# Value projections of a decoder trunk: two Strassen passes in place of one pass and direct products

## The chip, the cores and the metric

The kernel runs on one core of a Trainium2 chip. The metric is the device time of one execution in microseconds (us), as the median of several runs. Engines: TensorE (PE) multiplies, VectorE (DVE) and ScalarE (ACT) do the elementwise work, GpSimd (POOL) a little of it, SyncE (SP) issues most DMAs; ScalarE issues some as well. Each engine works through its own instructions in order.

## The reference, cut to what matters

One layer, 1024 tokens of 1024 channels, all in float32. A combined projection gives queries, keys and values of a differential attention (A: 4 heads, 512 value columns) and of three dilated window groups (B: 3 groups of 4 heads, 1536 value columns), and 2048 gate columns:

```
h    = rms_norm(x, pre_mix_g[l])
proj = h @ w_in[l]
qa, ka, va, qb, kb, vb, gates = jnp.split(proj, split_at, axis=-1)
...                                   # rope on q and k
oa   = diff_attention(qa, ka, va, lam)
outs, lses = dilated_group(qb[:, :, g], kb[:, :, g], vb[:, :, g], window, dil)   # g = 0, 1, 2
ob   = softmax of the lses over g, times outs
g_a, g_b = jnp.split(jax.nn.sigmoid(gates), 2, axis=-1)
mix  = (g_a * (norm(oa) @ w_a_out) + g_b * (ob @ w_b_out)) @ w_mix_out
x    = x + rms_norm(mix, post_mix_g[l])
```

A convolutional gated MLP with a second residual follows; the change leaves it alone.

## The kernel before, in words

**Products.** Every float32 matrix is split into a high part in TensorE's reduced float format (ScalarE copies it, name ending in `h` or `whi`) and a low part (VectorE subtracts, `l` or `wlo`). A product is then three matmuls, high times high, low times high and high times low (`mm3`, lines 153 to 156). So one block of 128x128 by 128x512 costs three matmuls of 128x512, one copy of the high part and one subtraction per weight tile.

**The x operand.** `xh` and `xl` hold x transposed, scaled by the norm's channel gain, as 8 chunks of 128 channels by 1024 tokens. The norm's own factor per token (`rstd`) is put in when results leave the PSUM banks.

**The start.** While x arrives in the order `K_FIRST` (chunks 0, 4, 1, 5, ...), PE does three of the sixteen gate projections, `FIRST_GATES`, k by k into six banks: 8 chunks x 6 banks x 3 = 144 matmuls of 128x512. Beside it VectorE and ScalarE form the sums of quadrants of x that Strassen's method needs (`sums_x`: t2, t3, t4 and the difference whose negative is b12).

**The Strassen pass.** For 1024 of the 2048 value columns (B groups 1 and 2) the 1024x1024 product of tokens and columns is done with seven products of halves, in Winograd's form (`order_v`: p1, p5, p6, p7, p3, p2, p4). A product is 4 steps, one for each k, of 12 matmuls; step n's weight (a quadrant of w_v or a sum of quadrants) is loaded 8 steps ahead (`fetch_v`), summed and split 5 steps ahead (`ready_v`). Quadrants and sums used again stay in the tiles `wa` and `wz`. Products take turns on the left banks (three `acc` and `o`) and the right ones (two `s` and two `pt`). After its last step, `take_v` (lines 497 to 512) copies or adds the four banks into the SBUF tiles `yv`, the four quarters of the result. These are scaled by `rstd` and stored to `v_d` in DRAM (`store_v`). During the pass the norm of x is computed (`norm_x`: 16 loads of raw x, 16 squares with a sum on ScalarE), and the rotary tables.

**The other 1024 value columns** (A, and B group 0) are projected directly by `proj_v` (lines 568 to 588): for 256 columns, 8 token tiles x 8 k x 3 = 192 matmuls of 128x256 (lines 577 to 579), four such calls. One runs in the start, after two more gates and the first head's projections; one in heads 1 and 2 of attention A, one in head 3 and one in the middle of B.

**Fill.** Attention steps wait for softmax, which is VectorE's and ScalarE's work. So `interleave` mixes other matmuls between them: a fill is a generator that gives up after every half unit, and it is spread over the jobs of a head by weight. `A_FILLS` names the fills of each A head: `p` and `P` the next projections of queries and keys, `g` one gate (48 matmuls), `v`, `w` and `V` the direct value projections. The B steps have the projections of the next step, and `ahead`, a value projection, in steps 4 and 5. The last `B_GATES` = 3 gates are fill after B.

**Order.** Engines run in the order in which a scheduler placed the program's instructions, and tiles come from pools with a fixed number of buffers, so a load waits until its buffer's last reader is done. All weight loads go through SP's queue in order; the stores of `v_d` through ScalarE's.

## Time and profile before

| what | value |
|---|---|
| median of 3 runs | 1745.36 us (1737.62 to 1745.58) |
| profiled execution | 1742.07 us, span 1740.3 us |
| mean granted TensorE clock | 0.992 |
| PE busy | 1709.9 us, 98% of the span |
| DVE busy | 1350.6 us, 78% |
| ACT busy | 886.3 us, 51% |
| DMA | 201.79 MB, mean 116 GB/s |
| raw loads of w_v | 24 of 256 KB |

The page gives busy times by engine and by group of instructions; a group's mean duration counts from issue to end, and since matmuls overlap, the sum of their durations is longer than the time they occupy. A window's row in the table by stages gives, for each engine, the time in which it had at least one instruction under way, with the number of instructions, then the clock granted to TensorE (1.00 is full), the share of DMA time and the rate in GB/s. An idle time is listed in brackets with what ended it.

### The profile page before, as it was taken

To read this page: it belongs to the slowest core of one execution; us is meant where nothing else is said; L and a number is where in the kernel's file an instruction comes from. 1 tells how busy PE (TensorE), PEld (TensorE's weight loads), DVE (VectorE), ACT (ScalarE), POOL (GpSimd) and SP (SyncE) were. 2 spreads that over 40 slices of the span, in tenths; PEclk is the share of its full clock that TensorE was granted. 3 is DMA by queue.
4 is the path that set the end of the run, shared out by engine and by line. 5 is a ranking of instruction groups with operands and counts; after the bars stand their busy time and mean duration, and the time that the engine had idled before them with its cause. 6 is when DMAs were issued, how large, how long until landed. Compare 5 with 4: busy or idle time off the path is not lost.

```text
span 1740.3 us, 23773 instructions
## 1 busy us (share of the span) xinstructions
PE 1709.9 (98%) x8510; PEld 1445.5 (83%) x8510; DVE 1350.6 (78%) x2642; ACT 886.3 (51%) x1629; POOL 54.4 (3%) x78
## 2 busy tenths in 40 slices
PE   9999999999999999999999999999999999999997
PEld 7878878898998888888877888878888888878886
DVE  8794677777757665777655767899999999789978
ACT  6654465555436674567652433354444444355452
POOL 1000000000000000000000500300000000000000
PEclk9999999999999999999999999999999999999999
DMA  5753101122112213422375532122222222196624
GB/s 208 237 182 123 53 26 66 56 80 90 38 62 73 84 51 117 153 85 74 123 267 189 185 119 98 37 91 97 79 97 79 79 91 97 56 345 209 206 79 157
DMA packets 103494, 201.79 MB, mean 116 GB/s; under 512 B 16768, under 2 KB 21568, under 8 KB 103376
## 3 DMA queue, kind: packets, MB, share of 16 engines
q1 hardware_dynamic: 97328, 189.26, 32.6%
q10 hardware_dynamic: 6048, 11.01, 1.7%
q8 instruction: 67, 1.10, 0.3%
q14 instruction: 51, 0.42, 0.1%
HBM read 156.57 MB, written 43.66 MB: 115 GB/s over the span
## 4 chain that ended last, share of the span: by engine, by line
PE 82%; DVE 7%; DMA 6%; ACT 2%; issue 2%; SPq 1%; POOL 0%; DVEq 0%; ACTq 0%; POOLq 0%
PE acc L155 16%; PE acc L154 16%; PE acc L156 16%; PE acc L1460 3%; PE acc L1459 3%; PE acc L1458 3%; PE o L634 2%; DMA og<-og_d 2%; PE pt L621 2%; PE acc L1139 2%; PE acc L1140 2%; PE acc L1138 2%; PE acc L578 2%; PE acc L577 2%; PE acc L579 2%
## 5 line engine op out<-in xcount | busy, mean ns | idle before, releaser
L154 PE MATMUL acc<-xh,whi 128*128 128x512 f32 x744 | 297.8, 401 | 6.2 <-ACT xh L358 2.6
L155 PE MATMUL acc<-xh,wlo 128*128 128x512 f32 x744 | 296.7, 399 | 0.9 <-DVE wlo L147 0.9
L156 PE MATMUL acc<-xl,whi 128*128 128x512 f32 x744 | 294.6, 398 | 0.0
L150 ACT ACTIVATE whi<-raw 128x512 fp32r<-128x512 f32 (+1 forms) x250 | 153.9, 624 | 226.3 <-PE acc L156 145.5
L147 DVE TENSOR_TENSOR wlo<-raw,whi 128x512 fp32r<-128x512 f32 (+1 forms) x247 | 174.7, 714 | 50.2 <-ACT whi L150 49.2
L154 PEld LDWEIGHTS acc<-xh,whi 128*128 128x128 f32 x744 | 141.3, 190 | 35.2 <-ACT xh L358 3.7
L155 PEld LDWEIGHTS acc<-xh,wlo 128*128 128x128 f32 x744 | 141.6, 190 | 27.9 <-DVE wlo L147 1.1
L156 PEld LDWEIGHTS acc<-xl,whi 128*128 128x128 f32 x744 | 141.5, 190 | 27.7
L154 PE MATMUL acc<-mh,whi 128*128 128x512 f32 x400 | 155.7, 390 | 0.3 <-ACT mh L150 0.2
L155 PE MATMUL acc<-mh,wlo 128*128 128x512 f32 x400 | 155.6, 389 | 0.0
L156 PE MATMUL acc<-ml,whi 128*128 128x512 f32 x400 | 155.4, 389 | 0.0
L608 ACT ACTIVATE t<-acc 64x512 f32<-64x512 f32 (+1 forms) x160 | 94.6, 591 | 47.9 <-PE acc L156 45.8
L1336 DVE TENSOR_TENSOR u<-acc,u 128x512 f32<-128x512 f32 x133 | 90.8, 687 | 26.4 <-PE acc L156 26.4
L150 ACT ACTIVATE whi<-s 128x512 fp32r<-128x512 f32 x76 | 47.0, 628 | 108.3 <-PE acc L156 96.0
L609 DVE TENSOR_TENSOR t<-acc,cos 128x512 f32<-128x512 f32 x64 | 44.1, 689 | 65.5 <-ACT t L608 63.2
L154 PEld LDWEIGHTS acc<-mh,whi 128*128 128x128 f32 x400 | 75.1, 188 | 16.2 <-ACT mh L150 0.5
L156 PEld LDWEIGHTS acc<-ml,whi 128*128 128x128 f32 x400 | 75.1, 188 | 15.6
L155 PEld LDWEIGHTS acc<-mh,wlo 128*128 128x128 f32 x400 | 75.1, 188 | 15.6
L1459 PE MATMUL acc<-whi,wlo 128*128 128x512 f32 x220 | 77.3, 389 | 0.0
L1458 PE MATMUL acc<-whi 128*128 128x512 f32 x220 | 75.8, 389 | 0.0
L578 PE MATMUL acc<-whi,xl 128*128 128x256 f32 x256 | 73.6, 288 | 0.0
L579 PE MATMUL acc<-wlo,xh 128*128 128x256 f32 x256 | 73.5, 287 | 0.0
(404 smaller groups left out, 4101.0 us busy)
## 6 DMA issues: line engine op xcount, KB each, us to landing
raw<-in_w_in SPq DMA_DIRECT2D x110, 256.0 KB, 2.7
raw<-in_w_up SPq DMA_DIRECT2D x88, 256.0 KB, 2.7
raw<-c_d SPq DMA_DIRECT2D x48, 256.0 KB, 3.3
c_d<-c SPq DMA_DIRECT2D x22, 512.0 KB, 2.7
raw<-in_w_down SPq DMA_DIRECT2D x37, 256.0 KB, 3.5
gl<-gt_d SPq DMA_DIRECT2D x16, 512.0 KB, 5.1
gt_d<-gate ACTq DMA_DIRECT2D x26, 256.0 KB, 2.4
raw<-in_w_v SPq DMA_DIRECT2D x24, 256.0 KB, 3.4
```

Source lines behind the costliest of these rows:

```text
L147: eng.tensor_tensor(lo, src, hi.bitcast(F32), op=ALU.subtract)
L150: nc.scalar.activation(hi, src, AF.Copy)
L154: nc.tensor.matmul(o, sh, mh, start=first, stop=False)
L155: nc.tensor.matmul(o, sl, mh, start=False, stop=False)
L156: nc.tensor.matmul(o, sh, ml, start=False, stop=last)
L578: nc.tensor.matmul(ps, xl[:, k, tk], wh[:, w], start=False, stop=False)
L579: nc.tensor.matmul(ps, xh[:, k, tk], wl[:, w], start=False, stop=k == KC - 1)
L608: nc.scalar.activation(t1[dst], ps[src], AF.Copy)
L1336: nc.vector.tensor_tensor(to, made(p), x, op=ALU.add)
L1458: nc.tensor.matmul(banks[m], gh[:, tk], wh, start=f == 0, stop=False)
L1459: nc.tensor.matmul(banks[m], gl[:, tk], wh, start=False, stop=False)
L1460: nc.tensor.matmul(banks[m], gh[:, tk], wl, start=False, stop=f == NH - 1)
```

## The change

- All 2048 value columns go through the Strassen method, in two passes (i = 0 and 1) of 1024 columns; `v_d` is twice as wide and holds them all. `proj_v` is gone, with its 768 matmuls of 128x256.
- The passes begin where the first gates stood: 12 steps of products p1 and p2 (p1 and p2 of pass 0 in turn, then p2 of pass 1), in the order in which the first chunks of x arrive. Then come p5, p6, p7, p4, p3 of pass 0, and p1, p5, p6, p7, p4, p3 of pass 1: 56 steps of 12 matmuls.
- Sums stay in the banks: the left banks go from p1 through p6 and p7 to p4 without being cleared, the right ones from p2 or p5 to p3. `take_v` copies the running sum out between two products, and the next product adds on top. Copies of p6, p7, p4 are ScalarE's; the rest is added by VectorE.
- No weight quadrant is kept in `wa`; each product loads what it needs, 72 raw loads of w_v in place of 24.
- The norm of x comes at step 16 (during p6 of pass 0), the rotary angles at 30, their tables at 53. Stores of pass 0 are at steps 26, 29, 33, 36; two quarters of pass 1 are stored through SP's queue.
- Attention reads all its values back from `v_d` (`fetch_values`, `split_values`): two tiles of 128x1024 with one split each for 256 columns.
- All sixteen gates are ordinary ones: one in the start, three in each A head (`A_FILLS`), three after B. `v`, `w` and `V` remain in the lists but hold no matmuls.

The core of the diff:

```diff
-START_GATES, A_FILLS, B_GATES = 2, ("gpgg", "pvgg", "wpgg", "PVg"), 3
+START_GATES, A_FILLS, B_GATES = 1, ("gpgg", "gpvgg", "wgpgg", "gPVgg"), 3
...
-FIRST_GATES = (0, 1, 2)
-XT_BUFS, NORM_AT, ANGLES_AT, STORE_AT = 6, 4, 18, 26
+XT_BUFS, NORM_AT, ANGLES_AT, TABLES_AT, STORE_AT = 6, 16, 30, 53, {26: 0, 29: 3, 33: 2, 36: 1}
...
-        order_v = (("p1", b11), ("p5", b12), ("p6", t2), ("p7", t3), ("p3", b22), ("p2", b21), ("p4", t4))
-        steps_v = [(p, x, k) for p, x in order_v for k in range(4)]
-        wa, wz = ([t[:, k % 2] for t in [q.tile([P, 2, 512], F32, tag=f"{n}{i}", name=n) for i in range(2)] for k in range(2)]
-                  for n, q in (("wa", first_w), ("wz", wv)))
-        ys_v = {(q, m): yv.tile([P, 512], F32, tag=f"y{q}{m}", name="yv") for q in range(4) for m in range(4)}
-        ready, got_v = {}, {}
+        xs_of = {"p1": b11, "p2": b21, "p5": b12, "p6": t2, "p7": t3, "p4": t4, "p3": b22}
+        steps_v = [(p, 0, k) for k in range(4) for p in ("p1", "p2")] + [("p2", 1, k) for k in range(4)]
+        steps_v += [(p, i, k) for i in range(2) for p in ("p1", "p5", "p6", "p7", "p4", "p3") if i or p != "p1" for k in range(4)]
+        wz = [t[:, k % 2] for t in [wv.tile([P, 2, 512], F32, tag=f"wz{i}", name="wz") for i in range(2)] for k in range(2)]
...
-        def w_at_v(i, j, k):
-            return a["w_v"][j * 4 + k][:, i * 512 : (i + 1) * 512]
+        def new_y(name, pool=None):
+            return [(pool or yv).tile([P, 512], F32, tag=f"y{name}{m}", name="yv") for m in range(4)]
         def fetch_v(n):
-            p, _, k = steps_v[n]
-            if p == "p1":
-                dma(wa[k], w_at_v(0, 0, k))
-            which = {"p5": ((1, 0), (1, 1)), "p7": ((1, 0),), "p3": ((0, 1),), "p2": ((0, 1),), "p4": ((1, 1),)}.get(p, ())
-            got_v[n] = [load_raw(w_at_v(i, j, k), next(tags)) for i, j in which]
+            p, i, k = steps_v[n]
+            which = {"p1": ((0, 0),), "p2": ((0, 1),), "p5": ((1, 0), (1, 1)), "p6": ((0, 0),), "p7": ((0, 0), (1, 0)),
+                     "p4": ((1, 1),), "p3": ((0, 1),)}[p]
+            got_v[n] = [load_raw(a["w_v"][j * 4 + k][:, (2 * i + c) * 512 : (2 * i + c + 1) * 512], next(tags))
+                        for c, j in which]
...
+        def take_v(p, i, m, ps):
+            y = ys_v[p, i][m] if (p, i) in ys_v else None
+            r0, r1 = (rstd[:, j * 4 + m : j * 4 + m + 1] for j in range(2))
+            def copy(to, r):
+                if i:
+                    nc.scalar.activation(to, ps, AF.Copy, scale=r)
+                else:
+                    nc.scalar.activation(to, ps, AF.Copy)
+            def add(to, r):
+                if i:
+                    plus(to, ps, r, to, ALU.add)
+                else:
+                    tt(to, ps, to, ALU.add)
+            if (p, i) in (("p1", 0), ("p2", 1)):
+                nc.scalar.activation(quarter[0, i][m], ps, AF.Copy)
+            if (p, i) in (("p1", 1), ("p2", 0)):
+                tt(quarter[0, i][m], ps, quarter[0, i][m], ALU.add)
             if p == "p6":
-                tt(c21, ps, c11, ALU.add)
-                tt(c12, c21, c22, ALU.add)
+                copy(quarter[1, i][m], r1)
             if p == "p7":
-                tt(c21, ps, c21, ALU.add)
-                tt(c22, c21, c22, ALU.add)
-            if p in ("p3", "p2", "p4"):
-                to = {"p3": c12, "p2": c11, "p4": c21}[p]
-                tt(to, ps, to, ALU.add)
-        def store_v(q, i, j):
+                copy(quarter[3, i][m], r1)
+            if p == "p4":
+                copy(quarter[2, i][m], r0)
+            if p == "p3":
+                add(quarter[1, i][m], r1)
...
+        def put_v(q, i, scale, queue):
+            c, j = q // 2, q % 2
             for m in range(4):
-                y, tk = ys_v[q, m], j * 4 + m
-                nc.scalar.activation(y, y, AF.Copy, scale=rstd[:, tk : tk + 1])
-                nc.scalar.dma_start(v_d[tk * P : (tk + 1) * P, i * 512 : (i + 1) * 512], y)
-        for k in range(4):
-            nt1 = t1_raw[k // 2][:, k % 2]
-            nc.scalar.activation(b12[0][:, k], nt1, AF.Copy, scale=-1.0)
-            nc.vector.scalar_tensor_tensor(b12[1][:, k], nt1, -1.0, f32(b12[0][:, k]), op0=ALU.mult, op1=ALU.subtract)
-        fetched = made = 0
-        for n, (p, x, k) in enumerate(steps_v):
+                y, tk = quarter[q, i][m], j * 4 + m
+                if scale:
+                    nc.scalar.activation(y, y, AF.Copy, scale=rstd[:, tk : tk + 1])
+                queue.dma_start(v_d[tk * P : (tk + 1) * P, (2 * i + c) * 512 : (2 * i + c + 1) * 512], y)
...
+        def step_v(n):
+            p, i, k = steps_v[n]
+            x = xs_of[p]
+            if p in ("p1", "p2", "p5") and k == 0:
+                left = p == "p1"
+                banks[left] = ([psum() for _ in range(3)] + [psum(F32, ps_o, "o")] if left else
+                               [psum(F32, q, t) for q, t in ((ps_s, "s"), (pt, "pt")) for _ in range(2)])
+            use = banks[p in ("p1", "p6", "p7", "p4")]
+            wh, wl = ready.pop(n)
+            for m in range(4):
+                tk = slice(m * P, (m + 1) * P)
+                mm3(use[m], x[0][:, k, tk], x[1][:, k, tk], wh, wl, k == 0 and p in ("p1", "p2", "p5"), k == 3, p in ("p6", "p7", "p4", "p3"))
+            if k < 3:
+                return
+            for m in range(4):
+                take_v(p, i, m, use[m])
+            if p == "p7":
+                for m in range(4):
+                    r, y = rstd[:, 4 + m : 5 + m], quarter[3, i][m]
+                    if i:
+                        plus(y, banks[False][m], r, y, ALU.add)
+                    else:
+                        tt(y, banks[False][m], y, ALU.add)
...
+            for j in range(KC):
+                fetch_v(j)
+                load_x(j, 0, 1 if j else 2)
+                if j:
+                    load_x(j - 1, 1)
+                w = 512 if j else 256
+                for c in range(0, 512, w):
+                    split_x(K_FIRST[j], slice(c, c + w), xts[j][:, c : c + w])
+                    if c == 0:
+                        ready_v(j)
+                if j % 2 and j > 2:
+                    sums_x(j // 2 - 1, xts[j - 3], xts[j - 2])
+            load_x(7, 1)
+            dma(cols, a["cols"])
+            dma(ghead, a["diff_head_g"])
+            nc.vector.tensor_scalar(ghead, ghead, 1.0 - LAM_INIT, None, op0=ALU.mult)
+            for n in range(8, 14):
+                fetch_v(n)
+            for n in range(8):
+                step_v(n)
+            for n in range(8, 10):
+                ready_v(n)
+            sums_x(3, xts[6], xts[7])
...
+            if n in STORE_AT:
+                put_v(STORE_AT[n], 0, True, nc.scalar)
+            if n == TABLES_AT:
+                make_tables(*args)
...
+            if k == 3 and i and p in ("p1", "p7", "p4"):
+                put_v({"p1": 0, "p7": 3, "p4": 2}[p], 1, p == "p1", nc.sync if p == "p7" else nc.scalar)
...
-    def proj_v(col, res, ms=range(8)):
...
+    def fetch_values(dil, c):
         n = S // dil // P
         src = v_d[:, c : c + 256].rearrange("(ih p r) c -> p r ih c", r=dil, ih=n)
-        for i in range(2):
-            v = slot("vperm", (P, 4, 256), F32)
+        vs = [slot("vperm", (P, 4, 256), F32) for _ in range(2)]
+        for i, v in enumerate(vs):
+            if dil == 1:
+                dma(v, src[:, 0, i * 4 : (i + 1) * 4])
+                continue
             for ih in range(n):
                 dma(v.rearrange("p (r ih) c -> p r ih c", ih=n)[:, :, ih], src[:, i * 4 // n : (i + 1) * 4 // n, ih])
-            h, l = v_tiles()
-            split(h, l, v)
-            res.append((h, l))
-            yield 0
+        return vs
+    def split_values(vs, res):
+        for v in vs:
+            res.append(v_tiles())
+            split(*res[-1], v)
...
-                "v": lambda: (proj_v(VA + 256, vs[1], range(4)), 4),
-                "w": lambda: (proj_v(VA + 256, vs[1], range(4, 8)), 4),
+                "v": lambda: (once(lambda: of_pair.extend(fetch_values(1, 256))), 0),
+                "w": lambda: (once(lambda: split_values(of_pair, vs[1])), 0),
...
-            fills.insert(0, (values_of(*nxt[:2]), 0))
-        elif h % 2:
-            fills.append((ahead, 4))
-        elif n + 2 < len(steps) and steps[n + 2][1] == 0:
-            ahead = values_of(*steps[n + 2][:2])
-            fills.append((itertools.islice(ahead, 8), 4))
+        if h % 2:
+            fills.insert(0, values_of(*nxt[:2]))
```

The order of the instructions shows how work moves at three places. The first is ScalarE around the norm of x: the squares (`raw,ssx<-raw`), the weights' high parts (`whi`) and the copies of banks (`yv`). Before, in a stretch of the pass where the copies belong to p5 on the right banks:

```order
L437 ACTIVATE raw,ssx<-raw 128x512
L150 ACTIVATE whi<-wz 128x512
L437 ACTIVATE raw,ssx<-raw 128x512 x4
L150 ACTIVATE whi<-wz 128x512
L437 ACTIVATE raw,ssx<-raw 128x512 x4
L503 ACTIVATE yv<-s 128x512
L437 ACTIVATE raw,ssx<-raw 128x512
L503 ACTIVATE yv<-s 128x512
```

In the changed kernel, from the last weights of p6 to the second copy of p6's sum:

```order
L145 ACTIVATE whi<-raw 128x512
L364 ACTIVATE raw,ssx<-raw 128x512
L145 ACTIVATE whi<-raw 128x512
L364 ACTIVATE raw,ssx<-raw 128x512 x4
L145 ACTIVATE whi<-raw 128x512
L364 ACTIVATE raw,ssx<-raw 128x512 x5
L444 ACTIVATE yv<-acc 128x512
L364 ACTIVATE raw,ssx<-raw 128x512
L444 ACTIVATE yv<-acc 128x512
```

Before, nine squares stand between two weights in two groups and four more alternate with the copies of p5, whose banks the product p6 does not use. Now ten squares stand ahead of the first copy of p6, and p7 goes on in the same banks.

The second place is PE at the hand-over from p6 to p7 of pass 0 (t2 is p6's operand, t3 p7's; the numbers tell tiles apart, acc_314 to acc_316 and o_317 are the left banks). In the changed kernel:

```order
L150 MATMUL o_317<-whi_635,t2h_116 128x512
L151 MATMUL o_317<-whi_635,t2l_117 128x512
L152 MATMUL o_317<-wlo_636,t2h_116 128x512
L150 MATMUL acc_314<-whi_656,t3h_118 128x512
L151 MATMUL acc_314<-whi_656,t3l_119 128x512
L152 MATMUL acc_314<-wlo_657,t3h_118 128x512
L150 MATMUL acc_314<-whi_751,t3h_118 128x512
L151 MATMUL acc_314<-whi_751,t3l_119 128x512
L152 MATMUL acc_314<-wlo_752,t3h_118 128x512
L150 MATMUL acc_314<-whi_770,t3h_118 128x512
```

p6 runs step by step through the four banks; p7 stays in one bank for its four steps, with four weights, before it takes the next.

The third place is PE in head 0 of attention A: scores `s<-k` and `s<-l`, turns `pt<-ident,s`, products with values `o<-pt`, sums of squares `o<-ones,sq`, and fill `acc<-xh` or `acc<-xl`. Before, the end of the head:

```order
L634 MATMUL o<-pt,vh 128x128 x2
L637 MATMUL o<-pt,vl 128x128
L637 MATMUL o<-pt,vl 128x256
L621 MATMUL pt<-ident,s 128x128
L762 MATMUL o<-ones,sq 128x1 x4
L621 MATMUL pt<-ident,s 128x128 x5
L689 MATMUL s<-k_1388,q_1386 128x256
L690 MATMUL s<-l_1390,q_1386 128x256
L154 MATMUL acc<-xh,whi 128x512
L155 MATMUL acc<-xh,wlo 128x512
L156 MATMUL acc<-xl,whi 128x512
```

and its last fill ahead of that is here:

```order
L154 MATMUL acc<-xh,whi 128x512
L155 MATMUL acc<-xh,wlo 128x512
L156 MATMUL acc<-xl,whi 128x512
L689 MATMUL s<-k_1387,q_1385 128x128
L690 MATMUL s<-l_1389,q_1385 128x128
L634 MATMUL o<-pt,vh 128x256
```

In the changed kernel the last fill comes earlier, here:

```order
L150 MATMUL acc<-xh,whi 128x512
L151 MATMUL acc<-xh,wlo 128x512
L152 MATMUL acc<-xl,whi 128x512
L150 MATMUL acc<-xh,whi 128x512
L619 MATMUL pt<-ident,s 128x128 x6
L687 MATMUL s<-k_1739,q_1737 128x128
L688 MATMUL s<-l_1741,q_1737 128x128
L151 MATMUL acc<-xh,wlo 128x512
L152 MATMUL acc<-xl,whi 128x512
L687 MATMUL s<-k_1738,q_1736 128x512
L688 MATMUL s<-l_1740,q_1736 128x512
L632 MATMUL o<-pt,vh 128x256
```

and the next is here, after the sums of squares:

```order
L619 MATMUL pt<-ident,s 128x128
L687 MATMUL s<-k_1738,q_1736 128x256
L688 MATMUL s<-l_1740,q_1736 128x256
L760 MATMUL o<-ones,sq 128x1 x4
L619 MATMUL pt<-ident,s 128x128 x5
L687 MATMUL s<-k_1739,q_1737 128x256
L688 MATMUL s<-l_1741,q_1737 128x256
L150 MATMUL acc<-xh,whi 128x512
L151 MATMUL acc<-xh,wlo 128x512
L152 MATMUL acc<-xl,whi 128x512
```

Before, the stretch without fill at the head's end holds the scores of two small blocks and the products of two; now it holds all scores and products of the last five blocks. In front of it, before, 120 matmuls of the start's direct value projection lie as fill among head 0's first blocks; they are gone.

266 lines of the change are left out of this document (96 added, 170 removed).

## The prediction

> **What bounds the kernel now.** I read the page's first two parts, then the table by stages, then PE's own timeline where that table shows PE short of its window.
>
> ```profile
> span 1740.3 us, 23773 instructions
> PE 1709.9 (98%) x8510; PEld 1445.5 (83%) x8510; DVE 1350.6 (78%) x2642; ACT 886.3 (51%) x1629; POOL 54.4 (3%) x78
> ```
>
> PE is busy for 98% of the span, so 30 us of idle time are all that better overlap could win; a larger gain has to come from fewer or cheaper matmuls. The stages that the change touches, with PE's busy time third in each row (after the window and its length) and the granted clock third from the end:
>
> ```profile
> 0.00:41.00 41.00, 37.19 (x145) 29.66 (x146) 33.95 (x52) 25.87 (x41) 6.82 (x9) 0.96 0.59 209
> 41.00:126.00 85.00, 82.76 (x363) 68.36 (x362) 69.07 (x119) 50.71 (x100) 2.50 (x2) 0.98 0.62 205
> 126.00:195.00 69.00, 69.00 (x397) 61.19 (x396) 35.22 (x65) 29.43 (x51) 0.00 (x0) 1.00 0.34 107
> 195.00:260.00 65.00, 62.72 (x319) 53.14 (x318) 46.20 (x133) 39.53 (x79) 0.00 (x0) 0.95 0.12 41
> 260.00:350.00 90.00, 88.42 (x504) 76.49 (x503) 70.13 (x196) 51.87 (x102) 0.00 (x0) 1.00 0.18 61
> 350.00:450.00 100.00, 100.00 (x564) 87.05 (x563) 77.13 (x221) 55.34 (x107) 0.00 (x0) 1.00 0.25 78
> 450.00:540.00 90.00, 90.00 (x584) 81.88 (x583) 59.70 (x175) 44.62 (x100) 1.14 (x4) 1.00 0.19 62
> ```
>
> 0 to 41 holds the three first gates, 41 to 126 the one Strassen pass, 126 to 195 the other gates of the start, the first projections and a direct value projection, 195 to 540 the four heads of attention A with their fill. PE is the bound in all of them: it loses 3.8 us in the first, 2.2 in the pass, nothing from 126 to 195, and in the heads 2.3 and 1.6 us plus 5% of clock in one window.
>
> **Removed and added matmuls.** The durations on the page overlap (matmuls are pipelined), so I price a matmul by how many start in a window that is full:
>
> ```profile
> 170.00:180.00 10.00, 10.00 (x83) 9.91 (x82) 9.24 (x15) 7.39 (x13) 0.00 (x0) 1.00 0.17 50
> 60.00:100.00 40.00, 40.00 (x178) 33.11 (x177) 29.52 (x61) 22.86 (x49) 2.50 (x2) 1.00 0.68 218
> L579 PE MATMUL acc<-wlo,xh 128*128 128x256 f32 x256 | 73.5, 287 | 0.0
> ```
>
> From 170 to 180 us only matmuls of 128x256 run: 10/83 = 0.1205 us each, where the group of one of the three lines gives 0.287. From 60 to 100 us only those of 128x512 run: 40/178 = 0.2247 us. The change removes all 768 matmuls of 128x256 (three lines with 256 each): 768 x 0.1205 = 92.5 us. It adds a second pass's 336 of 128x512: 336 x 0.2247 = 75.5 us. **Term: -17.0 us.** It is sure as far as PE stays full, since the order of the changed kernel's instructions shows these counts, and the stages it takes matmuls from (126 to 195, 350 to 450) have PE at 100%.
>
> [...]
>
> **The end of the pass.** PE's timeline and the chain of waits (start, length, what):
>
> ```profile
> 122.70 0.77 PE L154 MATMUL acc<-xh,whi 128*128 128x512 f32 x1 [2.24 <-DVE yv L299]
> 125.82 0.51 PE L155 MATMUL acc<-xh,wlo 128*128 128x512 f32 x1
> ```
> ```profile
> 115.92 4.59 DMA raw<-in_w_in
> 120.59 0.64 ACT whi L150
> 121.26 0.37 DVE wlo L147
> 121.87 0.69 DVE yv L299
> 122.70 0.77 PE acc L154
> ```
>
> The first gate after the pass needs the banks of the last product, which is on the left banks (`acc`). It waits 2.24 us for a DVE sum that stands behind the split of a late weight, and then the seven matmuls up to 125.82 take 3.12 us where 7 x 0.2247 = 1.57 are due: the clock is halved after the gap. In all 3.8 us. In the changed kernel the last product (p3) is on the right banks (`s` and `pt`), p4 left `acc` four steps earlier, and a gate can begin at once. **Term: -3.8 us**, bounds -3.8 (all of it goes) and 0 (the weight of the first gate, fetched behind the stores on SP, is late again).
>
> [...] I go by the row and charge 1.6 us of clock to any gap of about two microseconds.
>
> **The start.** 12 steps of the passes (144 matmuls) take the place of the 144 of the first gates, with the same x chunks behind them, so they end at about 42 us as now. What changes is what DVE must have done by then: the low halves of x, the sums for p5, p6, p7 and p4, and the weights' own low halves, 51 instructions by the order.
>
> ```profile
> 14.00:20.00 6.00, 6.00 (x28) 4.96 (x27) 6.00 (x9) 6.00 (x11) 5.00 (x2) 1.00 1.05 381
> 32.00:38.00 6.00, 6.00 (x28) 4.99 (x27) 6.00 (x11) 2.26 (x4) 0.00 (x0) 1.00 0.01 1
> ```
>
> In these windows DVE is full and does 9 and 11 instructions in 6 us each, 0.60 us apiece. 51 x 0.60 = 30.6 us; if DVE is full from 10 us on, p5's first weight is ready at about 41, one microsecond before PE asks. DMA has the bytes: the first 24 us need some 6.3 MB, and the row of 14 to 20 us shows 381 GB/s. **Term: +1.5 us**, bounds 0 and 4 (DVE begins or ends a few instructions later).
>
> **From p6 to p7.** Both products use the left banks, so before p7's first matmul into a bank ScalarE must copy p6's sum out of it. In ScalarE's order ten of the sixteen squares for the norm of x stand ahead of the first such copy, and it works in order.
>
> ```profile
> L437 ACT ACTIVATE raw<-raw x16: 613/626/638, 54.1 to 68.9; 128x512 f32<-128x512 f32 x16
> L437 ACT ACTIVATION_READ_ACCUMULATOR raw<-raw x16: 186/190/208, 54.7 to 69.5; 128x1 f32 x16
> ```
>
> A square takes 0.626 + 0.190 = 0.82 us, ten take 8.2. With a weight split and the copy itself (0.63 each) it is 9.4 us from the first square to a free bank. p5 and p6 are 96 matmuls, 21.6 us from 42, so PE arrives at 63.6. If the squares begin at 54.1 as now, the bank is free at 63.5: no wait. They need raw buffers that p7's weights (two loads a step) hold until DVE has split them; if that puts them at 58, the wait is 3.8 us and the clock's 1.6 come on top, 5.4 in all. PE does p7 bank by bank in the new order (2.7 us a bank), so only the first copy counts. **Term: +4 us**, bounds 0 and 8 (the copies themselves delayed by squares between them).
>
> **The other hand-overs on a chain** (p7 to p4, p1 to p6, p2 and p5 to p3, twice where there are two) each ask for one 0.63 us copy or one 0.68 us sum of a bank, with three other banks or a product on the other side to go on with. DVE and ScalarE have room (DVE 69.07 and ScalarE 50.71 of 85 us in the pass now). **Term: +2 us**, bounds 0 and 5. The 24 more raw loads of 256 KB that refetched weights need, and the values that now come back from DRAM as 128x1024 tiles with one split each, hide behind PE: the pass moves 205 GB/s now, against 381 shown. If that cover failed it would show as PE waiting for `whi`; I charge nothing.
>
> **Attention A.** The direct value projections were also fill: matmuls that PE does while softmax waits for DVE and ScalarE. Gates replace them in heads 1 to 3, in amounts nearly equal. In head 0 the old order has 120 matmuls of the start's value projection (14.5 us) as fill, and they have no successor: in the new order its last five blocks stand as one stretch without any fill, 11.9 us of PE work at the two matmul prices (pieces in proportion). Over the attention stages, stretches without fill of more than 1.5 us sum to 41.4 us in the old order and 63.7 in the new. What such a stretch costs now: in the windows from 195 to 540 PE lost 2.28 + 1.58 us of time and 5% of 65 us, 3.25, to the clock; 7.1 us for 41.4, 0.17 each. 22.3 more cost 3.8. **Term: +4 us**, bounds -3 (softmax keeps up, and head 0's present loss goes too) and +25 (the fourth rival's price). In the B heads the fill of 11.9 us at two steps goes; PE stands at 100% of the window from 350 to 450 and about it, and the projections of the next step remain as fill, so I charge nothing beside the matmuls; if they ran dry, it would be a few microseconds at each.
>
> **Sum.** -17.0 - 3.8 + 1.5 + 4 + 2 + 4 = -9.3 us. The profiled execution took 1742.07 us (span 1740.3), so the changed kernel should take 1732.8, **1733 us**. The median of the runs shown is 1745.36 (1737.62 to 1745.58), 3.3 above the profiled one; against it the forecast is 12.4 us or 0.7% less. About 0.5%, 8.7 us, is what a measurement of this kernel can tell from no change: faster means below 1736.6, slower above 1754.1.
>
> **Rivals.**
>
> 1. *More is gained.* DVE is ready at the start, the squares begin early and fill-less stretches are free: 1742.07 - 17.0 - 3.8 = 1721, and 1718 if head 0's present loss goes too. For it: PE at 100% in the window from 350 to 450 in spite of fill-less stretches. Against it: DVE's full windows from 14 to 38 and ten squares in front of a copy.
>
> 2. *The pass becomes bound by ScalarE and DVE.* All four uncertain terms at their upper bounds without attention's rise: -17.0 - 3.8 + 4 + 8 + 5 + 4 = +0.2, 1742; with the late weight still at the pass's end, 1746. For it: each product's start now waits for a copy or a sum that shares an engine with the weight splits, and the clock is halved after a gap. Against it: DVE's 69 of 85 us leave room, and most hand-overs have three banks to go on with.
>
> 3. *Halving the width halves the price.* If a matmul cost in proportion to its columns, 128x256 would be 0.1124 us, half of 0.2247, and the matmul term -86.3 + 75.5 = -10.8 in place of -17.0: 1739. The window from 170 to 180 us speaks against it, unless its 0.1205 holds waits that PE would have anyway. [...]
>
> 4. *Head 0 without fill decides, and the kernel is slower.* The place is the end of head 0, shown by PE's timeline of now:
>
> ```profile
> 246.94 1.05 PE L762 MATMUL o<-ones,sq 128*128 128x1 f32 x8 [1.03 <-ACT sq L754]
> 250.08 0.79 PE L154 MATMUL acc<-xh,whi 128*128 128x512 f32 x1 [1.25 <-DVE t L609]
> 255.37 0.58 PE L154 MATMUL acc<-xh,whi 128*128 128x512 f32 x1
> ```
>
> After a stretch of 4.5 us without fill PE waited 1.03 and 1.25 us, and then twelve matmuls took 5.29 us where 2.70 are due: 4.9 us lost, 1.1 for each fill-less one. At that price the 22.3 us cost 24.5 in place of 4, and the sum is +11.2: 1753. If the clock stays halved inside the 11.9 us too, its work takes that much longer: 1765. I put this rival at 1759, between the two; it ends above 1754.1 as soon as a fill-less microsecond costs 1.15. For it: the long stretch is three times the one that lost 4.9. Against it: other stretches as long as 5 us, in the windows after 260, lost under 2 us in all.
>
> That the change doesn't do what it says is hardly possible: the order shows all 672 pass matmuls and none of 128x256 in the projections.
>
> **Chances.** Forecast (1727 to 1736.6) 0.42; rival 1 (1717 to 1727) 0.22; rival 2 (1737 to 1754) 0.24; rival 3 0.02; rival 4 0.10. Faster is the first two, 0.64; within 0.5% rivals 2 and 3, 0.26; slower 0.10. The range leaves out rival 4, the far end of rival 2 and the best end of rival 1: 1719 to 1746.
>
> **What would show it.** In the profile after: no 128x256 group of 256 in the projections, and 128x512 at 0.225 us in full windows of the pass. The gap of 2.24 at the pass's end gone. A gap of up to 4 us before the first p7 matmul near 64 us, released by a ScalarE copy of `acc`; and one of about a microsecond near 42, released by DVE. PE in the window of head 0 short by some 4 us more than now; if it is short by 15 with a clock below 0.9, rival 4 holds. Wrong would be a DMA releaser in the pass (the refetched weights late), a clock that falls in the passes, or losses in the B heads.

## The result: slower, against the forecast

| | before | changed |
|---|---|---|
| median | 1744.42 us of 4 runs (1737.62 to 1745.58) | 1762.76 us of 4 runs (1761.60 to 1763.10) |
| span of the profiled execution | 1740.3 us | 1759.8 us |
| ratio | 1 | 1.0124, 95% interval 1.0103 to 1.0145 |

The forecast was 1733 us in a range of 1719 to 1746. The changed kernel is 1.2% slower, on the other side and outside of the range. The ratio and its interval are those of the fast runs on record; the two medians of the table alone would give 1.0105, which lies inside that interval.

The first two parts of the changed kernel's page:

```profile
span 1759.8 us, 23085 instructions
PE 1708.4 (97%) x8076; PEld 1421.5 (81%) x8076; DVE 1355.3 (77%) x2642; ACT 897.1 (51%) x1639; POOL 46.8 (3%) x75
```

434 fewer matmuls are there, and PE is busy for 1.5 us less only, though the matmuls taken away are worth 16 us by the table below. The mean granted clock fell from 0.992 to 0.984, about 14 us of the span, so the work that was taken away came back as half clock (after the wait at 33.09 us, for one, matmuls of 512 columns start 0.43 us apart up to 37.92, and 0.23 apart from 38.61 on); and 21 us more of PE's span are idle. The stages with a loss, first the passes, then the four A heads (columns as in the prediction's table):

```profile
0.00:42.00 42.00, 34.96 (x132) 27.36 (x133) 35.28 (x59) 28.34 (x48) 0.70 (x6) 0.92 0.76 244
42.00:60.00 18.00, 18.00 (x81) 14.88 (x80) 16.66 (x28) 10.56 (x20) 0.00 (x0) 1.00 0.48 157
60.00:80.00 20.00, 18.37 (x82) 14.88 (x81) 3.32 (x11) 14.10 (x39) 0.00 (x0) 1.00 0.74 235
80.00:130.00 50.00, 48.08 (x205) 39.02 (x204) 34.48 (x65) 27.15 (x48) 0.00 (x0) 0.97 0.79 254
130.00:165.00 35.00, 29.26 (x118) 23.62 (x117) 22.52 (x33) 16.73 (x25) 0.82 (x2) 0.90 0.49 162
...
255.00:300.00 45.00, 37.94 (x201) 31.64 (x200) 35.28 (x109) 25.69 (x56) 0.00 (x0) 0.89 0.12 43
300.00:380.00 80.00, 77.71 (x396) 65.70 (x395) 58.19 (x164) 45.14 (x88) 0.00 (x0) 0.96 0.21 69
380.00:460.00 80.00, 77.77 (x398) 65.87 (x397) 59.87 (x170) 42.36 (x85) 0.00 (x0) 0.96 0.20 61
460.00:550.00 90.00, 88.17 (x457) 75.03 (x456) 63.36 (x183) 37.92 (x78) 0.00 (x0) 0.98 0.24 81
```

To add idle time and half clock in one number I take, from all PE rows of the trace, how much later than plain cadence each matmul starts after the one before it, and sum where it is later. The cadence goes by the columns of the earlier one (0.227 us for 512 columns, 0.120 for 256, 0.173 for 384, 0.11 for smaller ones). This is the "loss over cadence" of the expectations too. By it:

| place | forecast of the change | loss before | loss after | difference |
|---|---|---|---|---|
| plain work of the matmuls | -17.0 | | | -16.1 |
| start, to 42 us | +1.5 | 8.2 | 11.7 | +3.5 |
| the passes and their end (42 to 126 before, 42 to 165 after) | -3.8 + 4 + 2 | 3.9 | 14.5 | +10.6 |
| the four A heads | +4 | 18.1 | 36.0 | +17.9 |
| all the rest | 0 | 32.7 | 33.5 | +0.8 |

The sum is +16.7 us; the missing 3 to the span's +19.5 are matmuls that follow closer than plain cadence, 24 us in all before and 21 after.

**In the A heads** the same pair of waits stands at the end of heads 0, 1 and 2; head 3 has the first of the two. PE's timeline and ScalarE's at the end of head 1:

```profile
360.29 1.05 PE L760 MATMUL o<-ones,sq 128*128 128x1 f32 x8 [1.03 <-ACT sq L752]
363.43 0.80 PE L150 MATMUL acc<-xh,whi 128*128 128x512 f32 x1 [1.25 <-DVE t L607]
```
```profile
359.60 0.63 ACT L752 ACTIVATE sq<-osb 128x512 f32<-128x512 f32 x1
360.26 2.39 ACT L606 ACTIVATE t<-acc 32x512 f32<-32x512 f32 x4
...
363.58 1.19 ACT L606 ACTIVATE t<-acc 32x512 f32<-32x512 f32 x2
```

`t<-acc` are the rotary copies that empty the banks of the next head's key projection. They stand on ScalarE directly behind `sq`, the squares of half a head's output, and these wait for the products of the head's late blocks. Until then two of the three `acc` banks are full, and PE does no fill from 355.7 to 363.4 us. In the kernel before, ScalarE in head 1 had begun all four copies at least 33 us ahead of the squares:

```profile
282.77 2.39 ACT L608 ACTIVATE t<-acc 32x512 f32<-32x512 f32 x4 [3.27 <-PE acc L156]
291.49 2.40 ACT L608 ACTIVATE t<-acc 32x512 f32<-32x512 f32 x4
295.55 2.39 ACT L608 ACTIVATE t<-acc 32x512 f32<-32x512 f32 x4 [1.00 <-PE acc L156]
305.11 2.40 ACT L608 ACTIVATE t<-acc 32x512 f32<-32x512 f32 x4
338.18 0.63 ACT L754 ACTIVATE sq<-osb 128x512 f32<-128x512 f32 x1
```

There the list of fills was `pvgg`, projections first; the change made it `gpvgg`. Only head 0 (`gpgg` in both) had the waits before; they are those at 246.94 and 250.08 that rival 4 quoted. The order alone does not make them: in head 2 of the kernel before (`wpgg`) two copies also came directly behind the squares (squares at 400.61, copies at 401.26 and 405.87), but PE had fill all the while, 25 matmuls of 512 columns from 400.6 to 408.3 us, and did not wait. It seems that such copies cost only at a time when PE has no other fill; no run tests that by itself.

**In the passes** the largest wait is at p6 to p7 of pass 1, and the one at the start is at the hand-over from p2 of pass 0 to p2 of pass 1. PE:

```profile
33.09 0.77 PE L150 MATMUL s<-whi,xh 128*128 128x512 f32 x1 [3.79 <-ACT whi L145]
...
145.34 0.79 PE L150 MATMUL acc<-whi,t3h 128*128 128x512 f32 x1 [5.74 <-ACT yv L442]
```

At 33 us the profile names a high part on ScalarE that ended at 33.01. That one is made from `wz`, a sum of quadrants as p5 needs it; p2 takes single quadrants (`raw`), whose low parts were done at 31.7. What p2 of pass 1 also needs is its bank `s`, which is free only when VectorE has added it to `yv`; the first of these adds ended at 32.95. VectorE, full, did them behind other work, of which these are the last instructions:

```profile
29.79 0.74 DVE L333 SCALAR_TENSOR_TENSOR cos<-xt,edge,cos 128x512 f32<-128x512 f32 x1
30.45 1.29 DVE L142 TENSOR_TENSOR wlo<-raw,whi 128x512 fp32r<-128x512 f32 x2
31.65 0.69 DVE L295 TENSOR_TENSOR wz<-raw 128x512 f32<-128x512 f32 x1
32.26 1.28 DVE L295 TENSOR_TENSOR yv<-s,yv 128x512 f32<-128x512 f32 x2
```

At 145 us ScalarE's copies of p6 stand behind p7's weights, these behind VectorE's differences (`raw<-raw`), and these behind the cosine's 1024-wide steps. Further back the chain of waits has 2.58 us of a load of x (`raw<-in_xT`), from 133.53. VectorE, then ScalarE:

```profile
138.66 1.22 DVE L315 SCALAR_TENSOR_TENSOR cos<-kk,cos 128x1024 f32<-128x1024 f32 x1
139.79 0.68 DVE L295 TENSOR_TENSOR raw<-raw 128x512 f32<-128x512 f32 x1
140.39 1.22 DVE L316 SCALAR_TENSOR_TENSOR cos<-kk,cos 128x1024 f32<-128x1024 f32 x1
141.63 0.69 DVE L295 TENSOR_TENSOR raw<-raw 128x512 f32<-128x512 f32 x1
```
```profile
142.42 1.15 ACT L145 ACTIVATE whi<-raw 128x512 fp32r<-128x512 f32 x2 [1.22 <-DVE raw L295]
143.56 1.15 ACT L370 ACTIVATE cos<-cos,edge 128x1024 f32<-128x1024 f32 x1
144.62 1.83 ACT L442 ACTIVATE yv<-acc,edge 128x512 f32<-128x512 f32 x3
```

### The profile page after: what moved, and what is told of

It reads as the page before. It is cut to its first block, busy times and chain, and to the rows that moved or that the text cites. A ratio compares the mean times of both kernels' runs of the same rounds, so it can differ in the third digit from the quotient of the medians.

```text
span 1759.8 us, 23085 instructions
## 1 busy us (share of the span) xinstructions
PE 1708.4 (97%) x8076; PEld 1421.5 (81%) x8076; DVE 1355.3 (77%) x2642; ACT 897.1 (51%) x1639; POOL 46.8 (3%) x75
## 4 chain that ended last, share of the span: by engine, by line
PE 76%; DVE 9%; DMA 8%; ACT 4%; issue 3%; SPq 0%; ACTq 0%; DVEq 0%
PE acc L150 17%; PE acc L151 17%; PE acc L152 17%; PE acc L1454 2%; PE acc L1455 2%; PE acc L1453 2%; DMA og<-og_d 2%; PE acc L1134 2%; PE acc L1133 2%; PE acc L1135 2%; PE o L632 2%; PE pt L619 1%; DMA raw<-in_w_v 1%; PE pt L1453 1%; PE pt L1454 1%
## 5 line engine op out<-in xcount | busy, mean ns | idle before, releaser
L150 PE MATMUL acc<-xh,whi 128*128 128x512 f32 x768 | 308.2, 401 | 3.7 <-DVE t L607 3.7
L152 PE MATMUL acc<-xl,whi 128*128 128x512 f32 x768 | 306.3, 399 | 0.0
L151 PE MATMUL acc<-xh,wlo 128*128 128x512 f32 x768 | 305.8, 398 | 0.0
L145 ACT ACTIVATE whi<-raw 128x512 fp32r<-128x512 f32 x251 | 155.2, 627 | 227.6 <-PE acc L152 142.0
L142 DVE TENSOR_TENSOR wlo<-raw,whi 128x512 fp32r<-128x512 f32 x251 | 178.3, 718 | 57.4 <-ACT whi L145 56.0
L150 PEld LDWEIGHTS acc<-xh,whi 128*128 128x128 f32 x768 | 146.5, 191 | 32.9 <-DVE t L607 4.4
L151 PEld LDWEIGHTS acc<-xh,wlo 128*128 128x128 f32 x768 | 146.4, 191 | 28.5
L152 PEld LDWEIGHTS acc<-xl,whi 128*128 128x128 f32 x768 | 146.2, 190 | 28.7
L1331 DVE TENSOR_TENSOR u<-acc,u 128x512 f32<-128x512 f32 x133 | 90.8, 686 | 23.5 <-PE acc L152 23.4
L1455 PE MATMUL acc<-wlo,whi 128*128 128x512 f32 x220 | 72.9, 389 | 0.0
L632 PE MATMUL o<-pt,vh 128*128 128x256 f32 (+1 forms) x376 | 69.6, 278 | 2.2 <-ACT pt L145 1.2
```

Source lines behind the costliest of these rows:

```text
L142: eng.tensor_tensor(lo, src, hi.bitcast(F32), op=ALU.subtract)
L145: nc.scalar.activation(hi, src, AF.Copy)
L150: nc.tensor.matmul(o, sh, mh, start=first, stop=False, skip_group_check=on)
L151: nc.tensor.matmul(o, sl, mh, start=False, stop=False, skip_group_check=on)
L152: nc.tensor.matmul(o, sh, ml, start=False, stop=last, skip_group_check=on)
L632: nc.tensor.matmul(o[:, q0 : q1 + 1], vs[b // 4][0][:, b % 4, c], t[:, part], start=first and n == part == 0, stop=False)
```

## The experiments

The ratios are to the kernel before, run on the same chip as each experiment (its medians there were 1737.7 to 1740.5 us). The passes are the same code in the changed kernel, a1 and a2; their gap at p6 to p7 of pass 0 was 1.79, 3.65 and 2.58 us over cadence in the three profiles, and at p6 to p7 of pass 1 it was 5.90, 7.37 and 7.01. So a single gap of the passes differs by some 2 us where nothing was done to it, and smaller changes of one gap say nothing.

### Four edits of the changed kernel, one at a time

**a1**, the order in the lists of fills:

```diff
-A_FILLS = ("gpgg", "gpvgg", "wgpgg", "gPVgg")
+A_FILLS = ("pggg", "pvggg", "wpggg", "PVggg")
```

> The changed kernel with one edit: in every A head the next projections come first in the list of fills, and then the gates (pggg, pvggg, wpggg, PVggg); the amounts stay. Theory K: in each head the key projection's evacuation (rotary copies on ScalarE) stands behind the sum of squares of the head's first half, holds two of the three acc banks meanwhile, and so stops the fill; with the projections first, all four copies come ahead of the squares, and PE's loss over plain matmul cadence in the A heads falls from 36 us to about 18 as in the kernel before: 1743 to 1749. Rival F (the amount of fill is too small, and its long stretch without fill sets the loss): the order shows 61.9 us of such stretches in place of 63.7, and 16.3 in place of 11.9 at the end of head 0, so no gain: 1758 to 1768.

Measured 1744.40 us, 1.0037 (1.0023 to 1.0052), where the changed kernel had 1.0124. The A heads of a1:

```profile
255.00:300.00 45.00, 39.06 (x203) 32.27 (x202) 31.18 (x110) 20.61 (x48) 0.00 (x0) 0.89 0.12 43
300.00:380.00 80.00, 79.01 (x416) 66.77 (x415) 63.52 (x177) 45.15 (x88) 0.00 (x0) 1.00 0.22 73
380.00:460.00 80.00, 79.56 (x421) 67.40 (x420) 60.57 (x171) 44.14 (x87) 0.00 (x0) 1.00 0.23 73
460.00:550.00 90.00, 90.00 (x475) 76.64 (x474) 58.35 (x171) 37.19 (x75) 1.64 (x4) 1.00 0.23 77
```

In head 1 ScalarE now has the last copies 22 us ahead of the squares:

```profile
338.20 2.39 ACT L606 ACTIVATE t<-acc 32x512 f32<-32x512 f32 x4
...
360.27 0.62 ACT L752 ACTIVATE sq<-osb 128x512 f32<-128x512 f32 x1
```

With the same amount of fill heads 1 to 3 lose 10.4 us in place of 22.2, and their clock is whole. Theory K holds for them. Head 0 still loses 14.0 (13.8), though its copies of K are now begun 46 us ahead of its squares: there K is not the cause. With that the four heads lose 24.6 us in all, more than the 18 of theory K.

**a2**, the gates after B moved into the heads (`A_FILLS` four gates each in heads 0 to 2, `B_GATES = 0`):

> The changed kernel with the three gates that are fill after B moved into the A heads 0, 1 and 2 (four each; none after B). Rival F (too little fill): 32.5 us more fill in the heads, of which up to 18 go into time that is lost now, so the A heads' loss falls by 12 to 18; what the last B step loses without fill is to be read from its window: 1747 to 1757. Theory K: only one of the four copies of K still stands behind the squares in head 0, others elsewhere; the loss falls by 4 to 8, and with a few us lost after B the time is 1757 to 1766.

1758.79 us, 1.0127 (1.0107 to 1.0147), no gain. The heads' loss does fall, from 36.0 to 22.3, but all that follows loses 44.2 us in place of 33.0, and the end of B, without its gates, 19.9 of them in one window of 75 us (860 to 935). The place of K's copies moved as well in this order, so a2 doesn't tell F from K; it shows that the gates after B earn there about what they would earn in the heads.

**a3**, `ANGLES_AT` 30 to 20, and **a4**, `STORE_AT` {26: 0, 29: 3, 33: 2, 36: 1} to {32: 0, 34: 3, 36: 2, 38: 1}:

> The changed kernel with the rotary angles at step 20 of the passes in place of step 30. Theory D: the 5.9 us gap and the half clock after it before p7 of pass 1 (8.7 us over cadence from 130 to 165) come from VectorE, which does 1024-wide angle instructions ahead of p7's weight differences, while ScalarE waits for these with the copies of p6 behind them; ten steps earlier VectorE is idle for 8 of 10 us, so the gap goes: 1753 to 1756. Rival R: the weights come too late anyway because six raw buffers hold everything that is loaded; the gap stays within 2 us: 1760 to 1763.

> The changed kernel with the four scaled stores of pass 0 at steps 32, 34, 36, 38 in place of 26, 29, 33, 36. Theory S: at 86 to 94 us ScalarE waits 7.95 us for the norm's rstd in front of the first scaled store, and p5's weights of pass 1 stand behind it; later stores end that wait, and the 3.9 us lost at 80 to 105 us go: 1758 to 1760. Rival R: VectorE itself waits 3.5 us there for a w_v load, so p5's first weight is as late as before: 1762 to 1764.

a3 took 1.0122 (1.0104 to 1.0140) and a4 1.0125 (1.0107 to 1.0142): neither is told from the changed kernel. (Their medians of 1759.36 and 1758.96 us are lower than its 1762.76 because the kernel before took 1737.67 beside them, and not 1744.42.) In a3 the gap at p6 to p7 of pass 1 shrank from 5.9 to 3.5 us over cadence; one of 1.7 came at 112 us, and the one at 70 us was 3.1. In a4 the 3.9 us at p3 to p5 are gone, and the gap at 70 us was 5.0. So theory S names a wait that goes when the stores move, theory D at most a part of one; the passes and their end still lose 13.1 and 13.2 us in place of 14.5.

### The same order put into the kernel before

**b1** does one part of the change alone, without any second pass:

```diff
-A_FILLS = ("gpgg", "pvgg", "wpgg", "PVg")
+A_FILLS = ("gpgg", "vpgg", "wpgg", "gPV")
```

> The kernel before with one edit: in A heads 1 and 3 the direct value projection, or a gate, comes first in the list of fills and the next projections second (vpgg and gPV in place of pvgg and PVg); the amounts stay. The order then has copies of K right behind the head's sum of squares in head 1, as in the changed kernel. Theory K: such a head loses about 4 us more, so 3 to 8 us in all: 1.002 to 1.005. Rival: with direct value projections as fill (smaller units of 1.4 us, half banks' chains of 2.9) it does no harm: 0.999 to 1.001.

1754.21 us, 1.0074 (1.0057 to 1.0091): more than theory K gave. Heads 1 to 3 of b1 and ScalarE in head 1:

```profile
260.00:350.00 90.00, 86.25 (x486) 75.10 (x485) 67.16 (x185) 48.37 (x96) 0.00 (x0) 0.98 0.18 63
350.00:450.00 100.00, 96.92 (x541) 84.42 (x540) 72.54 (x211) 51.34 (x101) 0.00 (x0) 0.98 0.21 69
450.00:540.00 90.00, 85.69 (x541) 77.28 (x540) 55.51 (x162) 40.77 (x89) 1.14 (x4) 0.98 0.13 45
```
```profile
324.82 0.63 ACT L754 ACTIVATE sq<-osb 128x512 f32<-128x512 f32 x1
325.48 2.39 ACT L608 ACTIVATE t<-acc 32x512 f32<-32x512 f32 x4
329.87 2.40 ACT L608 ACTIVATE t<-acc 32x512 f32<-32x512 f32 x4
```

The copies stand behind the squares again, and in these windows the heads lose 3.2, 4.6 and 6.1 us more; with 1.0 in head 0 that is 14.9 in all. So the position of the next projections among the fills costs the kernel before as much as it costs the changed one. The way there is not the same, though. PE waits longest at another instruction, in head 1 here and for 3.1 us each in heads 2 and 3:

```profile
339.25 0.65 PE L770 MATMUL pt<-ident,spread 128*128 128x128 f32 x4 [2.99 <-DVE spread L765]
```

`spread` is the norm's factor, which VectorE works out from the sums of squares; with late copies the rotary work on K stands between its steps. Head 2 has this wait too, although its list was not edited. So b1 shows what the order costs, and not that the banks held by the copies are the whole of it.

### Head 0

**c1** is a1 with the start's gate moved into head 0 (`START_GATES = 0`, head 0 `pgggg`):

> The changed kernel with the projections first in every A head's fills, as in the run a1 (1.0037 of the kernel before), and the start's one gate moved into head 0 as a fourth gate of fill. a1 still lost 14.0 us over cadence at the end of head 0. Theory F for head 0 (its fill is used up before its end): 10.8 us more fill there takes 7 to 11 of the 14 us: 0.997 to 1.000. Rival L (the loss is latency of head 0's own softmax chain, which fill would not reach because the scheduler uses it earlier): within 2 us of a1, 1.003 to 1.005; slower if the start misses its gate.

1741.29 us, 1.0002 (0.9990 to 1.0014). Head 0's loss fell to 10.8 only, 3.2 us less for 10.8 of fill, while the time fell by 0.0035, 6 us. The loss is between the two theories. **e1** asks the same in another way: the changed kernel with the direct projection that the start had before (192 matmuls of 128x256, its result unused), of which the order puts 120 into head 0:

> The changed kernel with an extra direct projection of 192 matmuls of 128x256 after the first head's projections, where the kernel before had one (23.1 us of PE work by 0.1205 us each; its result is written to scratch tiles and not used). The order puts 120 of them into head 0, as many as before. Theory F for head 0 (its 13.8 us of loss are fill that went away with the change): the loss at 255 to 300 us falls to about 7 or less, so the time grows by 13 to 17 us over the changed kernel (1.0124): 1.020 to 1.022. Rival L (head 0's loss has nothing to do with fill): it grows by the whole 23.1 us: 1.0255 to 1.027.

1774.51 us, 1.0199 (1.0173 to 1.0224): 0.0075 more than the changed kernel, so 23.1 us of work cost 13 us. Head 0's window in e1:

```profile
262.00:323.00 61.00, 56.71 (x299) 48.33 (x298) 44.99 (x119) 35.35 (x71) 0.00 (x0) 1.00 0.15 53
```

Its clock is whole where the changed kernel's is at 0.89, and it loses 6.4 us in place of 13.8. The other heads lose about as much as in the changed kernel (23.4 us, 22.2). The largest wait of head 0 in the changed kernel, 3.03 us for the softmax on VectorE, is gone in e1, where the largest is one of 2.95 us for `spread`; a1 still has it, with the same 3.03 us. In the changed kernel it is this line:

```profile
268.87 1.54 PE L619 MATMUL pt<-ident,s 128*128 128x128 f32 x6 [3.03 <-DVE s L705]
```

So head 0's part is the fill that the change took away. Why c1's gate did less for its length is not shown.

### The passes

**c2** (a1 with `NORM_AT` 12 in place of 16) and **c3** (a1 with the norm at 12, the angles at 20, the late stores, and the second halves of x reloaded during p4 of pass 1 in place of p5):

> As a1, with the norm of x at step 12 of the passes in place of 16. Theory Q: the gap before p7 of pass 0 (5.1 us over cadence from 60 to 80 in a1) is made by the squares that stand ahead of the copies of p6 on ScalarE; four steps earlier they are done before p6 ends and the 5.1 us go: 1.0005 to 1.0015. Rival R: the 16 loads of x share six raw buffers with the weights, so the weights of p6 and p7 come later instead and the gap turns up one product earlier or later: 1.003 to 1.005.

> As a1, with four edits in the passes together: norm at step 12, angles at step 20, scaled stores of pass 0 at 32, 34, 36, 38, and the second halves of x reloaded during p4 of pass 1 in place of p5. Theory: each gap of the passes is work for ScalarE or VectorE standing ahead of a bank's copy or a weight in an in-order queue; moved to where the queues are idle, the 14.4 us over cadence from 60 to 165 us in a1 fall below 5: 0.997 to 0.999. Rival R (raw buffers and DMA set the pace of the passes, whatever the order): 10 us or more stay: 1.002 to 1.005.

c2 took 1.0026 (1.0014 to 1.0037) and c3 1.0001 (0.9989 to 1.0012). In c2 the gap before p7 of pass 0 grew to 6.96 us: p7's weights now come late instead, as rival R had it, while the gap of pass 1 fell to 2.0. In c3 the loss at p6 to p7 of pass 1 fell from 9.3 to 0.1, and 11.3 of 14.4 us stayed, all in pass 0. So order alone can close the gap of pass 1, and in these two runs it did not mend pass 0. Which work it is that has to move is not singled out: c3 makes four edits at once, c2 took most of the loss of pass 1 away with the angles where they were (2.2 left of 9.3), and a3, which moved the angles alone, took 2.4 us of that gap. That the angles stand ahead of the copies is read from the timeline; how much they cost there by themselves stays open.

**d1** takes buffers away (raw loads of the passes through four in place of six), **d3** leaves out 14 of the norm's 16 loads and squares, both on a1:

> As a1 (1.0037 of the kernel before; 14.4 us lost over cadence from 60 to 165 us), with the raw loads of the passes cycling through four buffers in place of six. Theory R: in the passes each raw buffer's round (the load's 4.5 us, the wait behind other work, the split) is what paces weights and x, so the hand-overs p6 to p7 wait for whatever was loaded late; with two thirds of the buffers the loss in the passes grows by 10 us or more: 1.009 to 1.02. Rival Q (the order of work on ScalarE and VectorE alone): within 3 us of a1, 1.002 to 1.006.

> As a1, but 14 of the 16 loads and squares of x for the norm are left out (their sums are set to a constant), so the output differs by that. If the norm's loads and squares make the gap at p6 to p7 of pass 0 (5.1 us over cadence from 60 to 80 us in a1), it goes and nothing else: 1.000 to 1.002. If the gap is made by copies standing behind p7's weights (their loads paced by raw buffers), 3 us or more of it stay: 1.003 to 1.004. The gap in pass 1 (9.3 us) should stay in either case, since its work is the angles and the x reloads.

d1: 1.0056 (1.0038 to 1.0074), the passes lose 20.8 us in place of 14.4; less than theory R's 10, more than Q's 3. d3: 0.9995 (0.9979 to 1.0012); the passes lose 7.6, with 2.0 left at pass 0 and, against what I wrote, 5.6 in place of 9.3 in pass 1. So the norm costs about 7 us where it stands, in pass 1 as well as in pass 0, and d1 makes it likely that the buffers are a part of how.

**d2** (a1 with eight low halves on GpSimd) and **e2** (a1 with these eight subtractions left out):

> As a1, with the low halves of the sums t3 and t4 (eight subtractions of 128x512) made by GpSimd in place of VectorE. Theory V: the 3.95 us gap at 33 us, with half clock 5.6 us, is VectorE's throughput, which is full from 10 to 50 us with work that p5 doesn't need yet; some six of the eight subtractions leave its queue ahead of p5's weights, 6 x 0.6 = 3.6 us, so the gap shrinks to below 1 us: 0.999 to 1.001. Rival W: p5's weights themselves land late or VectorE slows down beside GpSimd, and the gap stays: 1.002 to 1.006.

> As a1 (1.0037), but VectorE's low halves of t3 and t4 are left out (eight subtractions of 128x512; the low tiles are zero, so p7 and p4 lose their low x part). Theory V: the 3.95 us gap at 33 us is VectorE's throughput; with some six subtractions less ahead of p5's weights (3.6 us) the gap falls below 1 us and its half clock with it: 4 to 5 us, 1.0005 to 1.0015. Rival W: p5's first weights are late for another reason (their loads, or sums that wait for PE in VectorE's queue): 1.003 to 1.005. That GpSimd's share in d2 made it slower would then be its own doing in both cases.

d2 took 1.0095 (1.0067 to 1.0122) and e2 1.0051 (1.0035 to 1.0068). Theory V falls: with six subtractions fewer the gap at 33 to 34 us stays at 3.68 us. VectorE has no idle time there in e2 either; in the new order other work has moved up ahead of the add that frees the bank. d2's larger gap, 6.34 us, names that add as its releaser. So it is the add's place in VectorE's queue, and not the amount of work, that I take to hold p2 of pass 1 up; no run moved the add alone. Why the gap at p6 to p7 of pass 0 was 9.26 us in d2 stays open. VectorE did slow down beside GpSimd there, as rival W had it: its two instructions of line 333 at 24.52 and 31.40 us, with a subtraction of GpSimd begun at 23.95 and at 31.23, took 1.78 and 1.77 us, and others like them in that trace 0.74.

**d4**, **e4**, **f1** and **f2** put together what helped. d4 is c1 with the angles at 20, the late stores and the late reload of x; e4 spreads the norm's loads over eight steps; f1 and f2 take them out of the raw buffers:

```diff
+            for m in range(8):
+                t = prep.tile([P, S], F32, tag="xt", name="xrow", bufs=XT_BUFS)
+                dma(t, a["x"][m * P : (m + 1) * P])        # f2: nc.gpsimd.dma_start
+                nc.scalar.activation(t, t, AF.Square, accum_out=ssx[:, m : m + 1])
```

> The edits that helped, together, with the norm left at step 16: projections first in the A heads' fills, the start's gate in head 0, angles at step 20, scaled stores of pass 0 at 32, 34, 36, 38, second halves of x reloaded during p4 of pass 1. If the gains of the single runs add up (0.0035 for the gate in head 0, 9 us for the gap of pass 1 that c3 closed), 0.993 to 0.996 of the kernel before; if what closes the one gap opens another, as the norm at step 12 did, 0.998 to 1.001.

> As d4 (0.9991), with the norm's 16 loads and squares spread, two a step, over steps 14 to 21 of the passes, so that none but two of them stands together ahead of a weight or a copy; angles at step 22. d3 showed that the loads and squares cost about 7 us where they stand. Theory: that cost comes from their coming all at once; spread out, the loss from 60 to 165 us falls from 6.5 to about 3: 0.996 to 0.998. Rival: six raw buffers carry 16 loads more in any case, and the gap only moves: 0.999 to 1.002.

> As d4 (0.9991), with the norm's squares taken out of the raw buffers: x is loaded as eight rows of 128x1024 into the six buffers that held x transposed, from SP's queue, right after p1 and p2's operands, and squared while the first products run. Theory: what the norm costs in the passes (d3: about 7 us with the fills of a1) is its 16 loads through the six raw buffers between weights, more than its squares; the gap at p6 to p7 of pass 0 (2.5 us over cadence in d4, 5.3 in c1) goes and the loss from 60 to 165 us falls to 2 to 3 us: 0.995 to 0.998. Rival: the x rows take SP's queue and ScalarE's time ahead of p5's weights, and the loss moves to 30 to 60 us: 0.999 to 1.002.

> As the run before it, with the eight loads issued by GpSimd, so that a load that waits for its buffer holds up no weight in SP's queue. Theory: as there, and the loads' waits cost nothing: 0.995 to 0.998, not slower than from SP. Rival: the buffers come free no sooner and what holds up p5 is VectorE's add of the right banks at 33 us in either case: equal to the run before within 0.001.

d4 0.9991 (0.9978 to 1.0004), e4 0.9987 (0.9974 to 1.0000), f1 0.9979 (0.9969 to 0.9989), f2 0.9978 (0.9968 to 0.9988). The gains of the single runs don't add up. In f1 the gaps at both p6 to p7 are gone, and a new loss of 6.8 us stands in p2 and p5, as its rival said; 2.8 us are lost from 80 to 130:

```profile
42.00:60.00 18.00, 14.61 (x51) 10.76 (x51) 14.43 (x26) 13.17 (x26) 0.00 (x0) 0.81 0.84 291
60.00:80.00 20.00, 19.99 (x88) 16.21 (x87) 13.43 (x34) 10.03 (x18) 0.00 (x0) 1.00 0.63 178
...
130.00:165.00 35.00, 35.00 (x156) 29.01 (x155) 19.43 (x30) 20.50 (x34) 0.82 (x2) 1.00 0.52 167
```

f1 and f2 beat both kernels: 0.2% faster than the one before, by intervals that leave out 1, and 1.4% faster than the changed one. The two don't differ, so taking the loads of the x rows off SP's queue gained nothing.

## Why the prediction was wrong

- **The matmul term** (-17.0 us) was right: the same counts at plain cadence give -16.1. The price from full windows held in the changed kernel (81 matmuls in the 18.00 us from 42 to 60, 0.222 each), and rival 3, with -10.8, did not.
- **The end of the pass** (-3.8) was right: no gap is left where the last product hands over to the gates; from 165 to 200 us the loss is 0.2.
- **The start** (+1.5, bounds 0 and 4): +3.5, inside, but at another place. I looked at p5's weights; the wait is at p2 to p2, for VectorE's add of the right banks. I had counted VectorE's work and not asked where in its queue the one instruction stands that frees a bank.
- **p6 to p7** (+4): in pass 0 the mechanism was as described, squares ahead of the copy, at 1.9 us from 60 to 80, and d3 bears it out (5.1 us in a1, 2.0 without most of the squares and loads). But pass 1 has a p6 to p7 too, and neither this term nor **the other hand-overs** (+2) lists it; it lost 8.7, and p3 to p5, not listed either, 3.9. I had reasoned that VectorE and ScalarE have room on average. In an in-order queue a copy waits for whatever stands ahead of it, and that was a chain through VectorE's angles and a DMA: in pass 1 p6's last matmul ended at 139.60 us, and ScalarE's first copy began at 144.62. The clock in the passes fell to 0.90 from 130 to 165 us, which the prediction had named as a sign of being wrong. This step was mis-sized: the passes and their end lost 10.6 us more than the pass before, where my three terms for them gave +2.2.
- **Attention A** (+4) is the step that failed: +17.9. I took the price of a fill-less microsecond from an average over stages, 0.17, of which 5.5 of 7.1 us came from the one head that had the costly waits; and I priced only the amount of fill. Of the loss, 11 us stand in heads 1 to 3, where the amounts were nearly equal, and a1 took them away by the order of the lists alone (22.2 to 10.4). I had stopped at equal amounts and did not ask which evacuation each list of fills puts behind the squares. The diff showed it in four strings. The other 7 us are in head 0, and they are missing fill (e1).
- **Rival 4** had the head's own price, which alone gave 1753, and stood at 1759 with the chance of 0.10. That it came near 1762.76 is in good part luck: its mechanism is right for head 0, explains nothing in heads 1 to 3, and has none of the 10.6 us of the passes.
- **The B heads and the rest** (0): +0.8, right.

With the projections first in the lists the changed kernel would have come out at 1.0037; the forecast of 0.993 needs much of the passes' and head 0's loss gone as well, and no run reached it (0.9978 in f2 was the lowest).

## What to carry to other kernels

When fill is exchanged, amounts are half of it: ask for each fill which engine's queue empties its bank, what stands ahead of that copy in the queue, and whether PE has other fill until then. Where work runs in banks that are handed on without a second set, the copy between two products is on the critical path (here PE waited 5.74 us for one), and everything queued ahead of it on that engine must be priced, however idle the engine is on average (here ScalarE was busy for 16.73 of the 35 us around that wait). And take the price of a wait from the place that has its pattern, never from an average over places that don't.
